# Seven products for a fourth quad of k tiles in the second pass of down, with splits in order of use and the LayerNorm's finishing steps put back

## The chip, the cores and the metric

The kernel runs on one core of one Trainium2 chip. The metric is the device time of one execution in microseconds (us). Below, PE is TensorE, DVE is VectorE, ACT is ScalarE, POOL is GpSimd and SP is SyncE; PEld is PE's loading of weights.

## The reference

One decoder layer on 256 tokens of width 2048, all in float32: a half-step FFN, a token mixer of two attention branches, a second half-step FFN, with a LayerNorm behind each. Cut to what matters here (D_MODEL 2048, D_FF 5632):

```python
def _swiglu(x, w_gate, w_up, w_down):
    return (jax.nn.silu(x @ w_gate) * (x @ w_up)) @ w_down

h = _layer_norm(ALPHA * h + 0.5 * _swiglu(h, ffn1_w_gate, ffn1_w_up, ffn1_w_down), ln1_g, ln1_b)
mix = _mixer(h, positions, ...)     # projections, MLA and differential attention, gates, w_out
h = _layer_norm(ALPHA * h + mix, ln2_g, ln2_b)
h = _layer_norm(ALPHA * h + 0.5 * _swiglu(h, ffn2_w_gate, ffn2_w_up, ffn2_w_down), ln3_g, ln3_b)
```

## The kernel before

**Three products for one.** Each float32 operand is split into a high part (a cast to `fp32r` by ACT, L150) and a low part (source minus high part, by DVE, L151). `triple` multiplies high by high (L203), high by the weight's low part (L204) and the activation's low part by the weight's high part (L205), each a PE instruction of 128 x 512, into one PSUM bank. Every weight tile is 128 x 1024 (two k tiles of 512 columns): one DMA from HBM into a `raw` or `sraw` tile, one cast and one subtraction into a pair of tiles called `wring`.

**The ring.** The `wring` pairs form a ring of six (four to five and more at other stages). `unit` queues a load, a preparation (the split) and the matmuls; `look(3, 4)` sets how many loads and how many splits stand ahead of the matmuls. A split can start only when the matmuls that read its pair before are done.

**Seven products.** Where two k tiles, two column halves and the two blocks of 128 tokens (b = 0, 1) can be taken as a 2 x 2 block product, seven products stand for eight, after Strassen's scheme. They need sums of weight tiles, made in place by DVE (`sraw<-sraw,sraw`, L392 in gate/up, L581 in down), and sums of activations (`f`, `xs`). In gate/up and in the mixer this is `Hybrid`, whose groups mix products of `sraw` tiles with plain units of `raw` tiles; `small` is the mixer's form of it. A group begins with product 1 on three pairs: `sraw`, `sraw`, `eraw`.

**Down.** The second matmul of the FFN has 44 k tiles, in 11 quads of four, and runs in two passes over the columns (p = 0, 1). `Sliced` takes some quads by seven products (seven units of one product, 6 matmuls each) and the others plainly (four units of 12 matmuls each). A string `mix` sets the order: `s` is a product, `p` a plain unit; eight plain units follow it. Before, quads 0 to 2 go by products in both passes. `QuadForms` holds a quad's split sums of `h`, `split_h` the plain splits of `h`. `hraw` tiles come from DRAM, where `turn_out` has written `h` transposed through `blocks` tiles.

**LayerNorm.** `evac` adds a bank to the row tile `z` (L729, L731) and takes its statistics (L734); after the last of four, `apply` aggregates them (L746), makes the inverse root (L645 to L662, the root itself on ACT, L647, with a table of functions to load first), and normalises the four pieces of `z` (L764, 128 x 512 each). PE transposes each piece (L633, to `tr`), ACT applies gain and bias by columns on the way out (L638) and casts to `h`: that is the input of the next stage. The rows for the residual get their gain and bias later, by DVE: the finishing steps L769 and L770, eight a block. `later(n, f)` calls `f` after n more units. The order in which the engines get their instructions is set by a scheduler that simulates the program's costs; `tc.issue_after(i)` keeps what is issued in its scope behind instruction i.

Of the kernel before, what the change touches and what calls it, by code (L numbers as in the profile page):

```python
# [59 lines left out]
def layer_kernel(ctx: ExitStack, tc: tile.TileContext, a: dict, out: bass.AP):  # L60
# [87 lines left out]

    def split(hi, lo, src):
        S.copy(hi, src)  # L150
        return V.tensor_tensor(out=lo, in0=src, in1=hi.bitcast(F32), op=ALU.subtract)  # L151
# [176 lines left out]

    class Hybrid:


        def __init__(self, x, seven, k_tiles, small=False, extra=None):

            self.x, self.seven, self.k_tiles, self.small, self.extra = x, seven, k_tiles, small, extra
            self.raws = {n: [act_tile([P, 1024], F32, "sraw") for _ in range(2)] for n in ("11", "12", "22")}
            self.raws["21"] = self.raws["12"] if small else [act_tile([P, 1024], F32, "sraw") for _ in range(2)]
            if extra is not None:
                for pair in (("11", "12"), ("22", "21")):
                    t = act_tile([P, 2, 512], F32, "eraw")
                    for i, n in enumerate(pair):  # L340
                        self.raws[n] = self.raws[n] + [t[:, i, :]]
            self.snaps = [act_tile([P, 2, 512], F32, "snap") for _ in range(2)]

        def group(self, w0, w1, done, wide=False, seeded=False):
# [36 lines left out]
            def seventh(p, s):  # L381
# [7 lines left out]
                def prep():  # L389
                    t = R[src][s]  # L390
                    if add is not None and (small or p != 7):
                        V.tensor_tensor(out=t, in0=t, in1=R[add[1]][s], op=ALU.add)  # L392
# [3 lines left out]
                    split(*pair, t)  # L396
# [16 lines left out]
            def plain(n, j, last=False):  # L413
# [8 lines left out]
                def prep():  # L422
                    pair = next_pair()
                    split(*pair, st["raw"])
                    st["pair"] = [v.rearrange("p (g n) -> p g n", g=G) for v in pair]

                def now():
# [7 lines left out]
                    if last:  # L435
                        done(1, 0, banks["Z"], n2, ALU.add)
                        done(1, 1, banks["X"], q5, ALU.add)
# [254 lines left out]
    class LayerNorm:  # L692
        def __init__(self, scale, residual, g, bt, each, x=None, cols=None, at=((0, 2, 4, 6), (8, 11, 14, 17))):
            self.scale = scale
            self.x = x
# [8 lines left out]
            self.gb = [[None, None] for _ in range(2)]  # L704

# [17 lines left out]
        def evac(self, c, b, bank):  # L723
            if c == 2 and b == 0:
                S.activation(sm(1, "sq"), zero[:, 0:1], AF.Sqrt)
# [18 lines left out]
        def apply(self, b):  # L744
# [18 lines left out]
            for c in range(4):  # L763
                V.tensor_scalar(out=zs[c], in0=zs[c], scalar1=mv[:, 0:1], scalar2=r,  # L764
                                op0=ALU.subtract, op1=ALU.mult)
                rows_to_quad(zs[c], b, self.x, c, *self.cols)

            def finish(c):
                V.tensor_tensor(out=zs[c], in0=zs[c], in1=gs[c], op=ALU.mult)  # L769
                V.tensor_tensor(out=zs[c], in0=zs[c], in1=bs[c], op=ALU.add)  # L770
                self.each(b, c, zs[c])
# [3 lines left out]
    def ffn(n, x, wgu, wdn, residual, g, bt, each, first=None, between=None, nxt=None, cols=None):  # L775
# [3 lines left out]
        def put_h(b, q):  # L779
            turn_out(hb[b, q], hT[q, b])  # L780

        def half(c, b, up, gate):
# [7 lines left out]
            if c % 2 == 1:  # L790
                later(2, lambda: put_h(b, q))
# [37 lines left out]
        def first_hook(j):  # L829
            if first is not None:  # L830
                first(j)
            if j == 5:
# [3 lines left out]
                between=between, behind_x=2 if n == 2 else None)  # L836
# [12 lines left out]
        ln = LayerNorm(0.5, residual, g, bt, each, nxt, cols, ((24, 26, 48, 50), (94, 97, 100, 103)))  # L849
# [3 lines left out]
        forms = {q: QuadForms(spare) for q in range(3)}  # L853
        down = Sliced(h_at)
# [5 lines left out]
        for p in range(2):  # L860
# [4 lines left out]
            else:  # L865
                kept = (9, 10)
                rest = deque(quad_units((9, 10, 3, 4)) + [(m, 2 * q + i) for m in range(2) for q in (5, 6, 7, 8) for i in range(2)])
                mix = "p" + "spspspspspspsppp" * 2 + "spspspspspss"
            products = deque((q, f, None) for q in range(3) for f in order)
# [7 lines left out]
            for q in range(3, KF // 4):  # L877
                first_use = min(i for i, u in enumerate(units) if len(u) == 2 and u[1] // 2 == q)
# [12 lines left out]
            else:  # L891
                call(len(units) - 8, widen)
# [507 lines left out]
```

## Time and profile before

| | |
|---|---|
| runs | 1984.77 us median of 3 (1983.05 to 1985.32) |
| profiled execution | 1982.88 us, its span 1981.1 |
| PE clock granted | 0.997 |
| sum of PE's idle time | 19.3 us |

The stages in the profiled execution: gate/up of the first FFN to about 440 us, down to 687 (its second pass from 572), the mixer to 1297, the second FFN to 1970, of which the second pass of down takes 1854 to 1970, and then the last LayerNorm. Times in profile lines are us from the span's start. In a timeline line the first number is the start, the second the duration; `x2` means two of the kind in a row; what stands in brackets is idle time before it and what ended it. In a line of the waits the numbers are the total, how many, and the longest. In a line of the windows stand the window, its length, the busy time of PE, PEld, DVE, ACT and POOL with their counts, the granted clock, the share of the DMA engines and GB/s. A PE instruction's duration goes on while the next has begun, so the pitch of matmuls is read from starts.

### The profile page before, as it was taken

The page shows a single profiled execution, that of the slowest core. Times are in us where ns is not written, and L with a number is a line of the kernel's source. Part 1 is how long each engine was busy: PE and PEld are TensorE (multiplying, and loading weights), DVE is VectorE, ACT ScalarE, POOL GpSimd, SP SyncE. Part 2 cuts the span into 40 slices and gives each one's busy share as a digit, 9 for nine tenths or more (in the row PEclk, how much of TensorE's full clock was granted, in tenths as well). Part 3 has the DMA queues.
Part 4 walks back from the last instruction along what each step waited for, and adds up shares of the span by engine and source line. Part 5 has one row for each costly group of instructions (what it writes and reads, how often), then busy time and mean ns, then how long its engine had stood idle before and what let it go on. Part 6 is the DMA issues. An engine that isn't in the chain of part 4 may idle for free.

```text
span 1981.1 us, 25579 instructions
## 1 busy us (share of the span) xinstructions
PE 1961.8 (99%) x8796; PEld 1623.6 (82%) x8796; DVE 1761.0 (89%) x2135; ACT 1269.4 (64%) x1639; POOL 294.6 (15%) x515
## 2 busy tenths in 40 slices
PE   9999999999999999999999999999999999999997
PEld 8888888888888897888888888878888888888886
DVE  7999999999898889998977686699999999998886
ACT  6666666677655666666667864566666666766552
POOL 0211112112100011002223130012112211121000
PEclk9999999999999999999999999999999999999999
DMA  8978888869677666677667677578898878687663
GB/s 314 284 241 279 284 238 247 239 212 329 244 235 243 202 243 225 226 254 260 217 198 256 216 236 264 185 256 271 244 290 260 247 239 244 208 325 251 238 215 124
DMA packets 144594, 484.63 MB, mean 245 GB/s; under 512 B 20640, under 2 KB 20688, under 8 KB 144464
## 3 DMA queue, kind: packets, MB, share of 16 engines
q1 hardware_dynamic: 112752, 389.60, 57.1%
q0 software_dynamic: 31712, 93.41, 17.9%
q8 instruction: 69, 1.13, 0.2%
q14 instruction: 61, 0.50, 0.1%
HBM read 454.08 MB, written 28.84 MB: 244 GB/s over the span
## 4 chain that ended last, share of the span: by engine, by line
PE 89%; DVE 6%; issue 3%; DMA 1%; POOL 0%; ACT 0%; SPq 0%; DVEq 0%; POOLq 0%; ACTq 0%
PE mm L204 28%; PE mm L205 28%; PE mm L203 28%; DVE wring L151 3%; DVE sraw L392 1%; PE tr L203 1%; PE tr L204 1%; PE tr L205 1%; DMA raw<-in_gu_dram 1%; PE tr L633 0%; DMA sraw<-in_wgm_dram 0%; PE tr L1134 0%; PE tr L1207 0%; PE tr L1209 0%; DMA hT<-blocks 0%
## 5 line engine op out<-in xcount | busy, mean ns | idle before, releaser
L150 ACT CAST wring<-raw 128x1024 fp32r<-128x1024 f32 (+2 forms) x475 | 491.4, 1038 | 344.9 <-PE mm L205 244.6
L151 DVE TENSOR_TENSOR wring<-raw,wring 128x1024 fp32r<-128x1024 f32 (+2 forms) x475 | 568.7, 1203 | 112.5 <-ACT wring L150 104.9
L150 ACT CAST wring<-sraw 128x1024 fp32r<-128x1024 f32 x436 | 455.4, 1052 | 207.7 <-PE mm L205 73.2
L151 DVE TENSOR_TENSOR wring<-sraw,wring 128x1024 fp32r<-128x1024 f32 x436 | 525.9, 1222 | 25.5 <-ACT wring L150 21.4
L205 PE MATMUL mm<-wring,h 128*128 128x512 f32 (+2 forms) x1260 | 485.0, 385 | 0.0
L203 PE MATMUL mm<-wring,h 128*128 128x512 f32 (+2 forms) x1260 | 484.7, 385 | 0.0
L204 PE MATMUL mm<-wring,h 128*128 128x512 f32 (+2 forms) x1260 | 484.6, 385 | 0.0
L204 PE MATMUL mm<-wring,xs 128*128 128x512 f32 x776 | 303.1, 391 | 2.5 <-DVE wring L151 2.4
L203 PE MATMUL mm<-wring,xs 128*128 128x512 f32 x776 | 302.3, 390 | 0.0
L205 PE MATMUL mm<-wring,xs 128*128 128x512 f32 x776 | 302.1, 389 | 0.0
L205 PEld LDWEIGHTS mm<-wring,h 128*128 128x128 f32 x1260 | 236.7, 188 | 47.4 <-DVE h L151 0.9
L203 PEld LDWEIGHTS mm<-wring,h 128*128 128x128 f32 x1260 | 236.9, 188 | 46.9 <-ACT h L150 0.4
L204 PEld LDWEIGHTS mm<-wring,h 128*128 128x128 f32 x1260 | 236.8, 188 | 46.9 <-DVE wring L151 0.3
L392 DVE TENSOR_TENSOR sraw<-sraw,sraw 128x1024 f32<-128x1024 f32 x168 | 203.3, 1220 | 3.5 <-DMA sraw<-in_wdv_dram 1.2
L204 PEld LDWEIGHTS mm<-wring,xs 128*128 128x128 f32 x776 | 145.6, 188 | 36.5 <-DVE wring L151 6.5
L203 PEld LDWEIGHTS mm<-wring,xs 128*128 128x128 f32 x776 | 145.7, 188 | 30.2
L205 PEld LDWEIGHTS mm<-wring,xs 128*128 128x128 f32 x776 | 145.7, 188 | 30.0
L204 PE MATMUL mm<-wring,x 128*128 128x512 f32 x348 | 135.7, 390 | 0.5 <-DVE wring L151 0.5
L203 PE MATMUL mm<-wring,x 128*128 128x512 f32 x348 | 135.7, 390 | 0.0
L205 PE MATMUL mm<-wring,x 128*128 128x512 f32 x348 | 135.2, 389 | 0.0
L394 POOL DMA_DIRECT2D sraw<-in_gu_dram x40 | 35.5, 887 | 579.0 <-DVE sraw L392 572.5
L670 POOL DMA_DIRECT2D hT<-blocks x176 | 97.2, 578 | 129.1 <-DVE blocks L668 117.6
(301 smaller groups left out, 2219.6 us busy)
## 6 DMA issues: line engine op xcount, KB each, us to landing
raw<-in_gu_dram SPq DMA_DIRECT2D x167, 512.0 KB, 4.9
sraw<-in_gu_dram SPq DMA_DIRECT2D x160, 512.0 KB, 5.1
raw<-in_dn_dram SPq DMA_DIRECT2D x140, 512.0 KB, 4.6
sraw<-in_gu_dram POOLq DMA_DIRECT2D x40, 512.0 KB, 5.5
sraw<-in_dn_dram SPq DMA_DIRECT2D x36, 512.0 KB, 5.4
hraw<-hT POOLq DMA_DIRECT2D x68, 256.0 KB, 5.3
raw<-in_w_out_dram SPq DMA_DIRECT2D x32, 512.0 KB, 4.4
eraw<-in_gu_dram SPq DMA_DIRECT2D x48, 256.0 KB, 5.1
```

Source lines behind the costliest of these rows:

```text
L150: S.copy(hi, src)
L151: return V.tensor_tensor(out=lo, in0=src, in1=hi.bitcast(F32), op=ALU.subtract)
L203: PE.matmul(o, xh, wh, start=first, stop=False, skip_group_check=again)
L204: PE.matmul(o, xh, wl, start=False, stop=False, skip_group_check=again)
L205: PE.matmul(o, xl, wh, start=False, stop=last, skip_group_check=again)
L392: V.tensor_tensor(out=t, in0=t, in1=R[add[1]][s], op=ALU.add)
L394: nc.gpsimd.dma_start(R["12"][s], source("22", s), accum_op=ALU.add)
L670: nc.gpsimd.dma_start(to.rearrange("(g r) (i f) -> i r g f", g=4, i=4)[i], t[32 * i:32 * (i + 1), :].rearrange("r (g f) -> r g f", g=4))
```

## The change

In the second pass of both downs the quad 3 (k tiles 12 to 15) goes by seven products as well. `mix` gets 28 products and 20 plain units for 21 and 24, in periods of 12 units for 16; with the eight at the end that is 56 units for 53. The forms of quad 3 are made in that pass, and those of quads 0 to 2 are given back behind their last product. Over the kernel PE has 12 matmuls of 512 columns fewer, DVE 28 instructions more (six splits and eight adds of 1024 columns among them), and ACT 26 table loads for 28.

The LayerNorm asks for the root's table ahead (`root_at` units after the second of the four evacuations of b = 1, behind the last cast). The finishing steps of both blocks stand behind the normalising step of b = 1 (`applied[1]`). In the hybrid groups outside the mixer each split stands behind the one before it (`split_in_line`), and the adds behind one or two of them; the writing out of `h` comes two units later and behind the last split.

```diff
+    line = []
+    def behind_split(n):
+        return tc.issue_after(line[-n].ins) if len(line) >= n else nullcontext()
+    def split_in_line(strict, *a):
+        with behind_split(1) if strict else nullcontext():
+            line.append(split(*a))
...
                     if add is not None and (small or p != 7):
-                        V.tensor_tensor(out=t, in0=t, in1=R[add[1]][s], op=ALU.add)
+                        with nullcontext() if small else behind_split(s + 1):
+                            V.tensor_tensor(out=t, in0=t, in1=R[add[1]][s], op=ALU.add)
...
-                    split(*pair, t)
+                    split_in_line(not small, *pair, t)
...
         def evac(self, c, b, bank):
-            if c == 2 and b == 0:
-                S.activation(sm(1, "sq"), zero[:, 0:1], AF.Sqrt)
+            def root_table():
+                with tc.issue_after(cast[0].ins):
+                    S.activation(sm(1, "sq"), zero[:, 0:1], AF.Sqrt)
+            if c == 1 and b == 1:
+                later(self.root_at, root_table)
...
             def finish(c):
-                V.tensor_tensor(out=zs[c], in0=zs[c], in1=gs[c], op=ALU.mult)
-                V.tensor_tensor(out=zs[c], in0=zs[c], in1=bs[c], op=ALU.add)
+                with tc.issue_after(self.applied[1].ins):
+                    V.tensor_tensor(out=zs[c], in0=zs[c], in1=gs[c], op=ALU.mult)
+                    V.tensor_tensor(out=zs[c], in0=zs[c], in1=bs[c], op=ALU.add)
...
             if c % 2 == 1:
-                later(2, lambda: put_h(b, q))
+                later(4, lambda: put_h(b, q))
...
-                between=between, behind_x=2 if n == 2 else None)
+                between=between, behind_x=3 if n == 2 else None)
...
+        late = (3,)
...
-                rest = deque(quad_units((9, 10, 3, 4)) + [(m, 2 * q + i) ...])
-                mix = "p" + "spspspspspspsppp" * 2 + "spspspspspss"
+                rest = deque(quad_units([q for q in (9, 10, 3, 4) if q not in late]) + [(m, 2 * q + i) ...])
+                mix = "p" + "sspspsspspsp" * 3 + "sspspspsps"
-            products = deque((q, f, None) for q in range(3) for f in order)
+            products = deque((q, f, None) for q in (range(3) if p == 0 else (0, 1, 2) + late) for f in order)
```

Three places show what moves. The first is DVE at the start of a gate/up group of the first FFN: adds and splits before, then the same after. `sraw` and `eraw` are the tiles of product 1, `raw_1155` is that of the plain unit behind it.

```order
L392 TENSOR_TENSOR sraw_460<-sraw_460,sraw_464 128x1024
L392 TENSOR_TENSOR sraw_461<-sraw_461,sraw_465 128x1024
L392 TENSOR_TENSOR eraw_468<-eraw_468,eraw_469 128x512
L151 TENSOR_TENSOR wring_121<-raw_1155,wring_120 128x1024
L151 TENSOR_TENSOR wring_115<-sraw_460,wring_114 128x1024
L151 TENSOR_TENSOR wring_105<-sraw_461,wring_104 128x1024
L151 TENSOR_TENSOR wring_103<-eraw_468,wring_102 128x512
```

```order
L405 TENSOR_TENSOR sraw_460<-sraw_460,sraw_464 128x1024
L405 TENSOR_TENSOR sraw_461<-sraw_461,sraw_465 128x1024
L405 TENSOR_TENSOR eraw_468<-eraw_468,eraw_469 128x512
L153 TENSOR_TENSOR wring_115<-sraw_460,wring_114 128x1024
L153 TENSOR_TENSOR wring_105<-sraw_461,wring_104 128x1024
L153 TENSOR_TENSOR wring_103<-eraw_468,wring_102 128x512
L153 TENSOR_TENSOR wring_121<-raw_1155,wring_120 128x1024
```

The split of `raw_1155` has moved from ahead of the three to behind them.

The second is DVE in the second LayerNorm, from the last evacuation of b = 1 (`z_9770`, after: `z_9784`) to the normalising step; `wring` rows are splits of the second FFN's first weights.

```order
L729 TENSOR_TENSOR z_9770<-mm_10163,z_9770 128x512
L151 TENSOR_TENSOR wring_105<-raw_10496,wring_104 128x1024
L734 BN_STATS bn_9643<-z_9770 128x6
L151 TENSOR_TENSOR wring_103<-raw_10517,wring_102 128x1024
L746 BN_AGGR mv_10359<-bn_9643 128x2
L770 TENSOR_TENSOR z_9664<-z_9664,gb_9913 128x512
L645 TENSOR_SCALAR ve_10361<-mv_10359 128x1
L769 TENSOR_TENSOR z_9735<-z_9735,gb_9863 128x512
L649 TENSOR_SCALAR w_10365<-mv_10359 128x1
L653 RECIPROCAL y_10367<-sd_10363 128x1
L770 TENSOR_TENSOR z_9735<-z_9735,gb_9966 128x512
L656 SCALAR_TENSOR_TENSOR t_10369<-y_10367,w_10365 128x1
```

```order
L749 TENSOR_TENSOR z_9784<-mm_10177,z_9784 128x512
L754 BN_STATS bn_9657<-z_9784 128x6
L153 TENSOR_TENSOR wring_117<-raw_10531,wring_116 128x1024
L766 BN_AGGR mv_10373<-bn_9657 128x2
L659 TENSOR_SCALAR ve_10375<-mv_10373 128x1
L663 TENSOR_SCALAR w_10379<-mv_10373 128x1
L667 RECIPROCAL y_10381<-sd_10377 128x1
L670 SCALAR_TENSOR_TENSOR t_10383<-y_10381,w_10379 128x1
L676 SCALAR_TENSOR_TENSOR f_10385<-t_10383,y_10381 128x1
L784 TENSOR_SCALAR z_9706<-z_9706,mv_10373,f_10385 128x512 x2
L784 TENSOR_SCALAR z_9784<-z_9784,mv_10373,f_10385 128x512 x2
L790 TENSOR_TENSOR z_9678<-z_9678,gb_9820 128x512 x2
```

The finishing steps (L769, L770) are gone from between the aggregate and the normalising step, and a split from ahead of the aggregate.

The third is DVE in the second pass of the first down, after: the third quad of products begins. `sraw_3452` is the tile that products 1, 5, 6 and 4 read and add to, `raw_4760` to `raw_4839` are plain units and the `21` tile; PE uses the pairs in the order `wring_105`, `103`, `121`, `119`, `117`, `115`.

```order
L153 TENSOR_TENSOR wring_105<-sraw_3452,wring_104 128x1024
L153 TENSOR_TENSOR wring_121<-raw_4760,wring_120 128x1024
L595 TENSOR_TENSOR sraw_3452<-sraw_3452,sraw_3453 128x1024
L153 TENSOR_TENSOR h_5028<-hraw_4925,h_5027 128x512
L595 TENSOR_TENSOR sraw_3453<-sraw_3453,sraw_3454 128x1024
L153 TENSOR_TENSOR wring_117<-raw_4794,wring_116 128x1024
L153 TENSOR_TENSOR wring_103<-sraw_3452,wring_102 128x1024
L153 TENSOR_TENSOR wring_115<-sraw_3453,wring_114 128x1024
L595 TENSOR_TENSOR sraw_3452<-sraw_3452,sraw_3454 128x1024
L153 TENSOR_TENSOR wring_105<-raw_4822,wring_104 128x1024
L153 TENSOR_TENSOR wring_103<-raw_4839,wring_102 128x1024
L153 TENSOR_TENSOR wring_119<-sraw_3452,wring_118 128x1024
```

The split of product 5 (`wring_103`) stands behind those of two later plain units, and the split of product 6 (`wring_119`) behind those of four pairs that PE uses later.

38 lines of the change are left out of this document (28 added, 10 removed).

## The prediction

> **What bounds the kernel now.** I read the page first, for the engine that carries the chain.
>
> ```profile
> span 1981.1 us, 25579 instructions
> PE 1961.8 (99%) x8796; PEld 1623.6 (82%) x8796; DVE 1761.0 (89%) x2135; ACT 1269.4 (64%) x1639; POOL 294.6 (15%) x515
> PE 89%; DVE 6%; issue 3%; DMA 1%; POOL 0%; ACT 0%; SPq 0%; DVEq 0%; POOLq 0%; ACTq 0%
> ```
>
> TensorE is the bound almost everywhere: only fewer matmuls, or fewer stalls of PE, can shorten the kernel. VectorE at 89% stands close behind, so whatever gives it work needs a look at the place where it lands. Next came the waits of PE, to see which stalls there are at all.
>
> ```profile
> PE tr L633 <- DVE z L764: 4.1, 1, 4.1
> PE mm L204 <- DVE wring L151: 3.0, 8, 1.3
> ```
>
> So there is one wait of 4.1 us for a LayerNorm's normalised rows, and eight for the low half of a weight split, the longest 1.3. The rest of the 19 us between PE's busy time and the span lies at the end, behind the last matmul, where the change leaves the last LayerNorm's work as it is. The third view is the timeline at those waits. This is the first of the eight, where a group of gate/up products begins; the columns are start, duration, engine and instruction.
>
> ```profile
> 142.56 1.22 DVE L151 TENSOR_TENSOR wring<-raw,wring 128x1024 fp32r<-128x1024 f32 x1
> 143.70 2.36 DVE L151 TENSOR_TENSOR wring<-sraw,wring 128x1024 fp32r<-128x1024 f32 x2
> 143.94 0.39 PE L204 MATMUL mm<-wring,x 128*128 128x512 f32 x1
> 144.17 0.39 PE L205 MATMUL mm<-wring,x 128*128 128x512 f32 x1
> 144.40 0.39 PE L203 MATMUL mm<-wring,xs 128*128 128x512 f32 x1
> 144.98 0.50 PE L204 MATMUL mm<-wring,xs 128*128 128x512 f32 x1 [0.19 <-DVE wring L151]
> 145.31 0.39 PE L205 MATMUL mm<-wring,xs 128*128 128x512 f32 x1
> ```
>
> Two prices come from it. A 512-column matmul lasts 0.39 us, but the next starts 0.23 later (143.94, 144.17, 144.40): I price matmuls by that pitch, 0.227 over longer stretches. A split of 1024 columns keeps VectorE for 1.14 (142.56 to 143.70). And the stall, shown as 0.19, costs more: 144.40 to 144.98 is 0.35 above the pitch, 144.98 to 145.31 another 0.10, so 0.45.
>
> **The matmuls.** Six PE instructions of 512 columns go with each b and k tile by the plain way, 48 for a quad; the seven products take 42. Two FFNs: 12 fewer, times 0.227 = **-2.7 us**, if PE stays the bound. By the full 0.39 it would be 4.7, a bound I don't use since starts are 0.23 apart.
>
> **Splits in order of use.** At 142.56 the split of a `raw` tile, which PE wants only after the seven's first products, runs ahead of the split of `sraw`, which PE waits for at 144.98. After the change the three `sraw` and `eraw` splits come first: theirs is done 1.14 us sooner, which is more than the 0.45 it came late. What it delays, the `raw` split, comes 2.9 us later (two splits of 1.14 and one of 0.6), at 146.7 instead of 143.8, and is wanted behind the 15 matmuls of the first product, at 144.40 + 0.45 + 15 x 0.227 = 148.3: it stays in time. Of the eight waits the longest, 1.3, belongs to the mixer's small group, whose order the change keeps. The seven others vanish: 7 x 0.45 = **-3.2 us**, 0 to -3.4. The adds that make the later products now stand in twos and threes behind the splits (2.3 to 3.4 us of VectorE in one piece); I cost that at nothing, since the ring keeps splits several us ahead there. If that cover were gone, each group would lose up to one add, 1.14.
>
> **The second LayerNorm.** These are VectorE and PE around the 4.1 us wait, then the window with its granted clock.
>
> ```profile
> 1288.94 0.69 DVE L729 TENSOR_TENSOR z<-mm,z 128x512 f32<-128x512 f32 x1
> 1292.59 0.26 DVE L746 BATCH_NORM_AGGREGATE mv<-bn 128x2 f32<-128x24 f32 x1
> 1292.76 0.63 DVE L770 TENSOR_TENSOR z<-z,gb 128x512 f32<-128x512 f32 x1
> 1296.15 1.92 DVE L764 TENSOR_SCALAR z<-z,mv,f 128x512 f32<-128x512 f32 x4
> 1299.31 1.29 DVE L769 TENSOR_TENSOR z<-z,gb 128x512 f32<-128x512 f32 x2
> ...
> 1292.29 0.39 PE L205 MATMUL mm<-wring,h 128*128 128x512 f32 x1
> 1296.75 3.37 PE L633 MATMUL tr<-ident,z 128*128 128x128 f32 x16 [4.07 <-DVE z L764]
> 1299.86 0.79 PE L203 MATMUL mm<-wring,h 128*128 128x512 f32 x1
> 1300.45 0.56 PE L204 MATMUL mm<-wring,h 128*128 128x512 f32 x1
> ...
> 1290.00:1300.00 10.00, 5.93 (x29) 4.60 (x27) 9.88 (x22) 3.90 (x10) 2.14 (x4) 0.87 0.77 279
> ...
> 685.32 0.20 ACT L647 ACTIVATE sd<-ve 128x1 f32<-128x1 f32 x1
> 686.21 1.92 DVE L764 TENSOR_SCALAR z<-z,mv,f 128x512 f32<-128x512 f32 x4
> ```
>
> From the last evacuation (1288.94) to the normalising step (1296.15) VectorE takes 7.2 us. Five finishing steps of the first block (gain and bias, L769 and L770) stand between the aggregate (1292.59) and the normalising step, 3.6 us later. The change puts them behind it; what is left is the root's own chain, 0.9 from the root to the normalising step where nothing is in between (the last two rows, of the first LayerNorm) and some 0.5 up to the root, an estimate from the short instructions around it: 1.4, so 2.2 less. One of the two splits between the evacuation and the aggregate is put ahead of both, another 1.1. So 7.2 becomes 3.9, and PE's wait of 4.1 becomes about 0.8. Behind the stall the clock is down: 0.87 over those ten us, and the first matmul at 1299.86 is followed only after 0.59. Without that another 0.7 goes, 0.4 of it in that gap. Together 4.0. The rule of the Trainium skill's page "TensorE: Matmul & The Clock Gate" (The HAM clock gate) says that an idle window of about 3.4 us halves the clock for about as long. The trace agrees with it, 4.07 us idle and then the lower clock; by that rule a wait of 0.8 would leave the clock up, as the sum has it.
>
> Not all of it can stay, for VectorE is busy without a pause until 1319 and the next weight splits are hardly ahead of PE:
>
> ```profile
> 1310.15 1.22 DVE L151 TENSOR_TENSOR wring<-raw,wring 128x1024 fp32r<-128x1024 f32 x1
> 1311.79 0.62 PE L204 MATMUL mm<-wring,h 128*128 128x512 f32 x2
> ```
>
> That split ends at 1311.37; the second of the two matmuls, which reads it, starts at 1312.01: 0.64 ahead. PE may come sooner by 0.64 plus what VectorE comes sooner. Before, 13 finishing steps stand between the evacuation and that split, after it 10, 0.60 each (two in 1.29 at 1299.31): 1.8, and the split put ahead 1.1. That makes 3.5, and less where an added instruction waits: I take **-3.2** (0 to -4.0). The six left over fall between later splits that have 4 us in hand.
>
> **The root's table.** In its first block the switch of tables stands in front of the root:
>
> ```profile
> 1273.67 1.28 ACT L647 ACT_TABLE_LOAD   x1
> ```
>
> PE has other matmuls there and no wait in the list above, so its 1.28 earlier costs and brings nothing. The page "ScalarE: Activation LUTs" of the Trainium skill (What ACT_TABLE_LOAD costs) has 1.28 us for the load too, but 2.66 with a drain; here the next instruction started at 1274.96, so no drain is seen, and by its figure too the saving would be hidden.
>
> **The first LayerNorm.** Here the change takes something away. Now four matmuls of the old pass and more stand between its transposes and the first use of `h`:
>
> ```profile
> 686.90 1.51 PE L633 MATMUL tr<-ident,z 128*128 128x128 f32 x12
> 688.16 0.48 PE L205 MATMUL mm<-wring,h 128*128 128x512 f32 x1
> 689.55 0.95 PE L203 MATMUL mm<-wring,h 128*128 128x512 f32 x2
> ...
> 687.57 1.51 ACT L638 ACTIVATE h1raw<-tr,cols 128x128 f32<-128x128 f32 x4 [0.16 <-PE tr L633]
> 689.30 0.64 ACT L150 CAST h<-h1raw 128x512 fp32r<-128x512 f32 x1
> ```
>
> ScalarE needs 3.0 us from the first transpose (686.90) to the end of the cast (689.94). After the change 16 transposes stand in one piece, 1.7 us by the 12 in 1.26 here, and the matmul that reads `h` is next: a wait of 1.3, and some 0.3 for the low half. The detours of now cost PE about 0.6 (689.55 and on): **+1.0** (0.3 to 2.0).
>
> **The fourth quad on VectorE.** In each second pass VectorE gets three splits and four adds of 1024 columns (7 x 1.14), four subtractions and its own splits of `h` less the plain ones, 2.3 together: 10.3 us. The quads of products also follow faster: 12 units where there were 16, 23.1 us of PE (7 products of 1.36, 5 plain of 2.72) for 34. The windows are the units before the last eight, of the first FFN and the second; below them are three splits there, and the matmuls that read them.
>
> ```profile
> 572.00:666.00 94.00, 94.00 (x417) 77.82 (x416) 84.97 (x105) 56.66 (x61) 4.37 (x8) 1.00 0.70 232
> 1854.00:1948.00 94.00, 94.00 (x417) 77.82 (x416) 80.97 (x81) 52.24 (x55) 4.25 (x8) 1.00 0.67 229
> ...
> 631.00 1.22 DVE L151 TENSOR_TENSOR wring<-raw,wring 128x1024 fp32r<-128x1024 f32 x1 [1.49 <-ACT wring L150]
> 636.02 1.22 DVE L151 TENSOR_TENSOR wring<-raw,wring 128x1024 fp32r<-128x1024 f32 x1
> 650.99 1.22 DVE L151 TENSOR_TENSOR wring<-raw,wring 128x1024 fp32r<-128x1024 f32 x1
> ...
> 640.82 0.39 PE L204 MATMUL mm<-wring,h 128*128 128x512 f32 x1
> 644.90 0.39 PE L204 MATMUL mm<-wring,h 128*128 128x512 f32 x1
> 657.14 0.39 PE L204 MATMUL mm<-wring,h 128*128 128x512 f32 x1
> ```
>
> VectorE would do 95.3 of 92.6 us in the first FFN, 91.3 in the second: it lives on its lead. The last quad of now is already packed as all will be, and there the lead falls from 7.7 (636.02, done 637.24, read 644.90) to 4.9 (done 652.21, read 657.14): 2.7 a quad. Four such quads use 10.8 of a lead of 7.7, so the first FFN comes 3.1 us short; the order of the change fits, for it puts the splits of later plain units ahead of those of two earlier products in the third quad. In the second VectorE has 4.0 less to do and just holds. **+3.1** (0 to 7).
>
> **Sum.** -2.7 - 3.2 - 3.2 + 1.0 + 3.1 = -5.0. The profiled execution took 1982.88 (span 1981.1 and 1.8 around it), so about 1977.9; the median of the runs lies 1.9 higher, so I say 1979.8.
>
> **Rivals.** *No new stall in the second pass*: the lead holds, as the 8.6 at 631.00 (done 632.22, read 640.82) and the 1.49 of idle before it suggest; -8.1, 1976.7. Against it stands VectorE's sum above PE's. *The LayerNorm gives nothing*: VectorE stays as late at 1310 as now, since the same finishing steps come in one piece before those splits; the 3.2 is lost, 1983.0. For it speaks the lead of 0.64, against it the three steps and the split that leave. *Slower: the second pass runs on VectorE in both FFNs.* If a quad costs 3.7 of lead, as from 631.00 to 650.99 (8.6 to 4.9), and from order and loads rather than load on VectorE, so that the second FFN pays too, the shortfall is 2 x (4 x 3.7 - 7.7) = 14.2, and -8.1 becomes +6.1: 1990.9. It is slower than before from a loss of 2.95 a quad on, and by over 0.2% from 3.45. Against it: the loss read over the nearer pair is 2.7, and VectorE has 13 us free in the second FFN.
>
> **Chances.** Forecast 0.46, no new stall 0.17, LayerNorm for nothing 0.17, slower 0.13, something else 0.07. A measurement of this kernel tells 0.2%, 4.0 us, from no change. Two thirds of the forecast's own spread, the second case and some of the rest lie below 1980.8: 0.53 faster. The rest of the forecast and the third case are within: 0.33. Slower 0.14. The range goes from 1975.0, the second case with the LayerNorm's 4.0 and the lower end of the first LayerNorm, to 1987.0, the third case with 4 us more in the second pass; half of the slower case and the odd ones are left out.
>
> **What would show it.** Right: no wait of PE for L151 at the groups' starts; PE's wait before the transposes near 1290 at 0.3 to 1.5, the granted clock there 1.00; a wait of 1 to 1.5 before the first `h` behind the first LayerNorm; PE waits for `wring` splits near 620 to 660 of some 3 us, none near 1900. Wrong: waits over 5 us in those passes, waits in the middle of the gate/up groups, or the first matmuls of the second FFN's gate held up by their splits for as long as the LayerNorm gained.

## The result and the profile after

The changed kernel takes **1995.4 us** (median of six runs, 1993.25 to 1996.95), the kernel before 1984.28 beside it: the ratio is 1.0057, with a 95% interval of 1.0047 to 1.0067. It is slower by 11 us, where 4.6 faster was forecast. The profiled execution took 1994.21, its span is 1992.4. (In the diff above the last part of `mix` lacks one letter; the program has "sspspsspsps".)

The page of after, with the engines and the chain:

```profile
span 1992.4 us, 25630 instructions
PE 1964.7 (99%) x8784; PEld 1623.6 (81%) x8784; DVE 1774.8 (89%) x2163; ACT 1268.0 (64%) x1649; POOL 294.3 (15%) x515
PE 80%; DVE 11%; issue 4%; DMA 3%; ACT 1%; POOL 0%; SPq 0%; DVEq 0%; ACTq 0%; POOLq 0%
```

PE has its 12 matmuls fewer and yet is busy 3 us longer: some of them ran at a lower clock. The chain has moved by 9% of the span from PE to DVE, issue and DMA. PE's waits in after:

```profile
PE tr L647 <- DVE z L784: 5.0, 2, 4.6
PE tr L206 <- DVE wring L153: 4.2, 2, 2.4
PE mm L206 <- DVE wring L153: 2.8, 5, 1.2
PE tr L205 <- ACT wring L152: 1.8, 1, 1.8
```

The wait of 4 us for a LayerNorm's rows is still there, but at another LayerNorm. New are the waits of `tr` matmuls, which are products of the second pass of down.

**The second pass of the first FFN.** The timeline of after there, first PE, then ScalarE and VectorE, then SyncE's issue of loads, then the window:

```profile
624.83 0.49 PE L205 MATMUL tr<-wring,xs 128*128 128x512 f32 x1 [1.83 <-ACT wring L152]
627.76 0.80 PE L206 MATMUL tr<-wring,xs 128*128 128x512 f32 x1 [2.44 <-DVE wring L153]
628.36 0.63 PE L207 MATMUL tr<-wring,xs 128*128 128x512 f32 x1
628.78 0.63 PE L205 MATMUL tr<-wring,xs 128*128 128x512 f32 x1
...
619.12 1.05 ACT L152 CAST wring<-sraw 128x1024 fp32r<-128x1024 f32 x1 [6.27 <-DMA sraw<-in_dn_dram]
623.73 1.04 ACT L152 CAST wring<-sraw 128x1024 fp32r<-128x1024 f32 x1 [0.62 <-DVE sraw L595]
...
611.06 2.35 DVE L153 TENSOR_TENSOR wring<-sraw,wring 128x1024 fp32r<-128x1024 f32 x2
620.20 1.23 DVE L153 TENSOR_TENSOR wring<-sraw,wring 128x1024 fp32r<-128x1024 f32 x1 [2.58 <-ACT wring L152]
622.48 1.22 DVE L595 TENSOR_TENSOR sraw<-sraw,sraw 128x1024 f32<-128x1024 f32 x1
624.22 1.22 DVE L595 TENSOR_TENSOR sraw<-sraw,sraw 128x1024 f32<-128x1024 f32 x1
625.35 1.22 DVE L153 TENSOR_TENSOR wring<-raw,wring 128x1024 fp32r<-128x1024 f32 x1
626.49 2.35 DVE L153 TENSOR_TENSOR wring<-sraw,wring 128x1024 fp32r<-128x1024 f32 x2
...
612.30 1.46 SPq L590 DMA_DIRECT2D sraw<-in_dn_dram  x2
...
606.00:640.00 34.00, 29.73 (x119) 23.78 (x118) 28.19 (x34) 17.76 (x22) 2.12 (x4) 0.90 0.69 243
```

Read it from the load. One tile holds block 11 of the weights, and products 1, 5, 6 and 4 use it in turn, adding to it in place. The next quad's load can be issued only when the split for product 4 is done, at 612.30; the cast for the next product 1 waits 6.27 us on ScalarE and starts at 619.12, 6.8 after the issue. PE reaches that product just as its split ends (621.4), so the load has cost it nothing yet. What it waits for is the next product, 5: its add follows only at 622.48, and PE waits 1.8 for the cast behind that add (623.73); then an add for product 7 (624.22) and the split of a plain unit (625.35) stand in VectorE's line ahead of its split (626.49), and PE waits 2.4. So the late load takes away the lead, and the order that the third view of the change showed, six us from product 1's split to product 5's, then lies open. VectorE is not short of time here: in the window it is busy 28.19 of 34 us. Behind 4.3 us of waiting the matmuls come 0.43 apart for a while (628.36, 628.78) instead of 0.23: the granted clock in that window is 0.90, before it was 1.00. The waits cost 4.7 us of PE's starts and the lower clock 2.5: 7.2 there. In the second FFN the same place costs 4.0, with one wait, and matmuls 0.43 apart behind it:

```profile
1916.17 0.66 PE L206 MATMUL tr<-wring,xs 128*128 128x512 f32 x1 [1.80 <-DVE wring L153]
1916.62 0.63 PE L207 MATMUL tr<-wring,xs 128*128 128x512 f32 x1
1917.05 0.63 PE L205 MATMUL tr<-wring,xs 128*128 128x512 f32 x1
```

**The first LayerNorm.** The same three engines:

```profile
698.84 3.80 PE L647 MATMUL tr<-ident,z 128*128 128x128 f32 x16 [4.64 <-DVE z L784]
702.69 0.79 PE L205 MATMUL mm<-wring,h 128*128 128x512 f32 x1
...
693.26 1.05 ACT L152 CAST wring<-raw 128x1024 fp32r<-128x1024 f32 x1 [3.69 <-DMA raw<-in_wc_dram]
694.22 0.19 ACT L661 ACTIVATE sd<-ve 128x1 f32<-128x1 f32 x1
...
691.40 0.15 DVE L663 TENSOR_SCALAR w<-mv 128x1 f32<-128x1 f32 x1
694.34 1.23 DVE L153 TENSOR_TENSOR wring<-raw,wring 128x1024 fp32r<-128x1024 f32 x1 [2.80 <-ACT wring L152]
695.49 0.15 DVE L667 RECIPROCAL y<-sd 128x1 f32<-128x1 f32 x1
698.15 1.91 DVE L784 TENSOR_SCALAR z<-z,mv,f 128x512 f32<-128x512 f32 x4
```

The root (694.22) stands on ScalarE behind the cast of a tile of `in_wc`, the mixer's first weights, which waits 3.69 for its load. VectorE then runs three splits of that matrix between the root's steps. So a weight that PE wants much later holds up the LayerNorm for which PE is waiting, and after 4.64 us of idle PE runs at half clock again (16 transposes in 3.80, the first matmuls 0.59 and 0.43 apart).

**The second LayerNorm** did what was forecast:

```profile
1305.47 0.39 PE L207 MATMUL mm<-wring,h 128*128 128x512 f32 x1
1306.25 1.57 PE L647 MATMUL tr<-ident,z 128*128 128x128 f32 x12 [0.39 <-DVE z L784]
1308.51 0.66 PE L647 MATMUL tr<-ident,z 128*128 128x128 f32 x4 [0.69 <-ACT h2raw L652]
1309.36 0.50 PE L205 MATMUL mm<-wring,h 128*128 128x512 f32 x1 [0.20 <-ACT h L152]
```

The wait is 0.39 for 4.07, and PE's last matmul of the mixer to the first of the FFN takes 3.9 us (1305.47 to 1309.36) for 7.6 (1292.29 to 1299.86): 3.7 gained.

Where the 11 us are, from PE's times at the same instructions in both traces: gate/up of the first FFN -0.1, its second pass of down +6 (7.2 less 1.4 of matmuls), the first LayerNorm +7, the mixer +0.5, the second LayerNorm -3.7, gate/up of the second FFN -0.2, its pass +2.6 (4.0 less 1.4), the rest -0.5: 11.3 together.

### The profile page after: what moved, and what is told of

Same layout as the page of the kernel before. It is cut to its first block, busy times and chain, and to the rows that moved or that the text cites. A ratio compares the mean times of both kernels' runs of the same rounds, so it can differ in the third digit from the quotient of the medians.

```text
span 1992.4 us, 25630 instructions
## 1 busy us (share of the span) xinstructions
PE 1964.7 (99%) x8784; PEld 1623.6 (81%) x8784; DVE 1774.8 (89%) x2163; ACT 1268.0 (64%) x1649; POOL 294.3 (15%) x515
## 4 chain that ended last, share of the span: by engine, by line
PE 80%; DVE 11%; issue 4%; DMA 3%; ACT 1%; POOL 0%; SPq 0%; DVEq 0%; ACTq 0%; POOLq 0%
PE mm L206 25%; PE mm L207 25%; PE mm L205 25%; DVE wring L153 6%; DMA sraw<-in_dn_dram 2%; DVE sraw L405 1%; ACT wring L152 1%; DVE sraw L595 1%; PE tr L206 1%; PE tr L207 1%; DMA raw<-in_wc_dram 1%; PE tr L205 1%; DVE blocks L682 1%; PE tr L647 0%; DMA sraw<-in_wgm_dram 0%
## 5 line engine op out<-in xcount | busy, mean ns | idle before, releaser
L152 ACT CAST wring<-raw 128x1024 fp32r<-128x1024 f32 (+2 forms) x469 | 483.6, 1037 | 316.8 <-PE mm L207 204.6
L153 DVE TENSOR_TENSOR wring<-raw,wring 128x1024 fp32r<-128x1024 f32 (+2 forms) x469 | 559.4, 1199 | 104.7 <-ACT wring L152 103.1
L152 ACT CAST wring<-sraw 128x1024 fp32r<-128x1024 f32 x448 | 464.3, 1051 | 232.5 <-DVE sraw L405 77.7
L153 DVE TENSOR_TENSOR wring<-sraw,wring 128x1024 fp32r<-128x1024 f32 x448 | 535.5, 1218 | 40.5 <-ACT wring L152 39.3
L205 PE MATMUL mm<-wring,h 128*128 128x512 f32 (+2 forms) x1228 | 472.9, 386 | 0.2 <-ACT h L152 0.2
L207 PE MATMUL mm<-wring,h 128*128 128x512 f32 (+2 forms) x1228 | 473.1, 386 | 0.0
L206 PE MATMUL mm<-wring,h 128*128 128x512 f32 (+2 forms) x1228 | 472.9, 385 | 0.0
L206 PE MATMUL mm<-wring,xs 128*128 128x512 f32 x792 | 309.1, 390 | 2.7 <-DVE wring L153 2.0
L205 PE MATMUL mm<-wring,xs 128*128 128x512 f32 x792 | 308.5, 389 | 0.0
L207 PE MATMUL mm<-wring,xs 128*128 128x512 f32 x792 | 308.3, 389 | 0.0
L206 PEld LDWEIGHTS mm<-wring,h 128*128 128x128 f32 x1228 | 231.6, 189 | 46.6 <-DVE wring L153 1.1
L205 PEld LDWEIGHTS mm<-wring,h 128*128 128x128 f32 x1228 | 231.6, 189 | 46.4 <-ACT h L152 0.9
L207 PEld LDWEIGHTS mm<-wring,h 128*128 128x128 f32 x1228 | 231.2, 188 | 46.1 <-DVE h L153 0.5
L206 PEld LDWEIGHTS mm<-wring,xs 128*128 128x128 f32 x792 | 148.7, 188 | 36.8 <-DVE wring L153 6.1
L205 PEld LDWEIGHTS mm<-wring,xs 128*128 128x128 f32 x792 | 148.6, 188 | 30.9
L207 PEld LDWEIGHTS mm<-wring,xs 128*128 128x128 f32 x792 | 148.7, 188 | 30.6
```

The lines of the kernel that those rows point to most:

```text
L152: cast[0] = S.copy(hi, src)
L205: PE.matmul(o, xh, wh, start=first, stop=False, skip_group_check=again)
L206: PE.matmul(o, xh, wl, start=False, stop=False, skip_group_check=again)
L207: PE.matmul(o, xl, wh, start=False, stop=last, skip_group_check=again)
```

## The experiments

The times are medians, each ratio to the kernel before on the same chip. Theory R, the reload of shared tiles, and its rivals are told in the expectations.

| run | us | ratio, 95% interval |
|---|---|---|
| changed kernel | 1995.4 | 1.0057 (1.0047 to 1.0067) |
| e1 without the fourth quad | 1981.9 | 0.9991 (0.9982 to 1.0001) |
| e2 the fourth quad alone | 1995.9 | 1.0057 (1.0042 to 1.0072) |
| e3 two tiles for block 11 | 1993.1 | 1.0041 (1.0026 to 1.0056) |
| e4 splits free | 1995.9 | 1.0060 (1.0045 to 1.0075) |
| e5 two tiles for each block | 1987.0 | 1.0014 (1.0005 to 1.0023) |
| e6 one tile, gap in the order | 1986.1 | 1.0011 (1.0002 to 1.0021) |
| e7 LayerNorm part alone | 1982.7 | 0.9993 (0.9984 to 1.0002) |
| e8 no fourth quad, adds free | 1984.3 | 0.9998 (0.9989 to 1.0007) |
| e9 mixer's splits behind the LayerNorm | 1994.6 | 1.0052 (1.0035 to 1.0069) |
| e10 e6 with e9 | 1987.0 | 1.0019 (1.0010 to 1.0029) |
| e11 e5 with e6's order and e9 | 1986.3 | 1.0015 (1.0005 to 1.0025) |
| e12 fourth quad in the second FFN alone | 1982.5 | 0.9990 (0.9980 to 0.9999) |

**Which part it is.** e1 takes the quad out of the changed kernel, e2 puts it alone into the kernel before, with the making of its forms, and e4 frees the splits.

```diff
# e1, and for e2 the other way round in the kernel before
-        late = (3,)
+        late = ()
...
-                mix = "p" + "sspspsspspsp" * 3 + "sspspsspsps"
+                mix = "p" + "spspspspspspsppp" * 2 + "spspspspspss"
# e4
     def behind_split(n):
-        return tc.issue_after(line[-n].ins) if len(line) >= n else nullcontext()
+        return nullcontext()
...
-                later(4, lambda: put_h(b, q))
+                later(2, lambda: put_h(b, q))
...
-                between=between, behind_x=3 if n == 2 else None)
+                between=between, behind_x=2 if n == 2 else None)
```

> The changed kernel with the second pass of down as before (quad 3 plain, the old mix). Theory R (reload): the loss comes from the fourth quad, since the one tile that products 1, 5, 6 and 4 share is reloaded while PE waits, and the first LayerNorm's wait of 4.6 us follows from the lead lost there. Then this kernel has no wait in either second pass, under 1.5 us at the first LayerNorm, keeps the 3.7 us won at the second, and takes 1980 to 1982. Theory N (norm): the first LayerNorm's wait comes from the finishing steps and the table put elsewhere; then the wait of 4.6 and the half clock behind it stay, and it takes 1988 to 1990.

> The kernel before with the second pass of down alone changed (quad 3 by products, the new mix). Theory R: waits of 4 to 5 us near 620 and of 2 near 1910, with half clock behind them, and a wait at the first LayerNorm of some us; 1984.3 - 2.7 + 8 + 4 + up to 8, so 1993 to 2001. Theory N: the waits of the passes alone, no new one at the first LayerNorm: 1992 to 1994.

> The changed kernel without the order of splits (splits, adds and the writing out of h free for the scheduler, as before). By the prediction that order is worth 3.2 us: 1998.6. By the trace of after each group's stall only went from 0.45 to 0.28, because the adds start later by about as much as the split came forward: 0.5 to 1 us, 1995.4 to 1996.5, and less certain, for the scheduler may move other places.

e1 gave 1981.9, e2 1995.9: the quad alone is worth a loss of some 12 us, and the rest of the change is hardly 2 faster, a gain that e1's interval does not yet tell from none. Theory N as it was put is out: with the finishing steps put back but no quad, PE waits for normalised rows 0.9 us at two LayerNorms together, 0.5 at most. In e2 the first LayerNorm's wait is 1.4, and the second's 4.3 is kept. That e2 and the changed kernel take the same time is therefore chance: by PE's times at the same instructions e2 loses 7.4 in the first pass, 1.2 at the first LayerNorm and 3.9 in the second FFN's pass, the changed kernel 6.0, 6.8 and 2.6, less what it gains at the second LayerNorm. At the first LayerNorm the quad alone costs 1.2, the LayerNorm part without the quad (e1, e7) 1.3 to 1.7, both together 6.8.

```profile
PE mm L206 <- DVE wring L153: 2.8, 5, 1.2
PE tr L647 <- DVE z L784: 0.9, 2, 0.5
PE tr L647 <- ACT h1raw L652: 0.7, 1, 0.7
```

These are e1's waits; no `tr` matmul waits in the pass. e4 is as slow as the changed kernel: its time shows no worth of the order of splits, though intervals of 3 us to either side hardly rule out the 3.2 that I gave it. The traces do: gate/up of both FFNs takes 0.9 longer in e4, and 0.7 of that is one wait at 1719.

**The tiles.** e3 and e5 give a block a second tile, e6 keeps one and moves plain units.

```diff
# e5 (e3: for "11" alone)
-            self.R = {n: act_tile([P, 1024], F32, "sraw") for n in ("11", "12", "22")}
+            self.R = {n: [act_tile([P, 1024], F32, "sraw") for _ in range(2)] for n in ("11", "12", "22")}
...
-                        nc.sync.dma_start(R[load_block], w[j])
+                        nc.sync.dma_start(R[load_block][q % 2], w[j])
# e6
-                mix = "p" + "sspspsspspsp" * 3 + "sspspsspsps"
+                mix = "p" + "sspsspsssppp" * 3 + "sspsspsspps"
```

> The changed kernel with two tiles for the shared operand (block 11), used by turns, so that the next quad's load doesn't wait for the last add of the quad before. Theory R: both passes' waits and their half clock go (8 and 4 us), the lead at the pass's end is back to several us and the first LayerNorm's wait falls below 2: 1976 to 1980. Theory V (VectorE's work): the tile is not what binds, VectorE's 10.3 us more per pass is; then PE still waits for wring splits in the first FFN, and the time stays above 1990.

> The changed kernel with two tiles for each of the three blocks (11, 12, 22) that the products share, used by turns. Theory R2 (one tile each is too few for quads that follow every 23 us: with two for block 11 alone the wait moved on to block 22, where an add waited 2.7 us for its load): no wait over 0.6 in either pass, no half clock there, the first LayerNorm's wait at most 1: 1977 to 1981. Theory V (VectorE, or the load on DMA): waits of several us at wring splits stay in the first FFN, 1988 to 1993.

> The changed kernel with one tile each and the same units, in another order: products 1, 5, plain, 6, 7, plain, 2, 4, 3 and then three plain units, so that PE has 10.9 us instead of 8.2 between product 4 and the next product 1, and 15.0 instead of 9.5 between 3 and the next 6. Theory R2: the reload of either tile is hidden again, the waits in the passes go or fall below 1 us each, and it takes 1977 to 1983. Theory V: the work of VectorE, of ScalarE and of DMA is the same to the last instruction, so the waits stay and it takes 1990 to 1996.

e3 took the waits at 622 away and got another, 20 us earlier. VectorE in e3, an add for product 7 that waits for block 22's load, and PE's longest wait:

```profile
600.74 1.23 DVE L602 TENSOR_TENSOR sraw<-sraw,sraw 128x1024 f32<-128x1024 f32 x1 [2.67 <-DMA sraw<-in_dn_dram]
PE tr L206 <- DVE wring L153: 5.8, 5, 3.7
```

It is block 22's turn: products 6, 7 and 3 share that tile, and product 5's split, for which PE waits 3.7, stands behind that add in VectorE's line. The pass costs as much as in the changed kernel, 6.2 more than before. With two tiles for every block (e5) PE works through the first FFN's pass without a pause, VectorE as busy as it can be. Its windows over that pass:

```profile
572.00:606.00 34.00, 34.00 (x152) 28.15 (x151) 33.97 (x53) 21.76 (x23) 2.12 (x4) 1.00 0.61 204
606.00:640.00 34.00, 34.00 (x152) 28.15 (x151) 33.97 (x41) 24.99 (x32) 3.19 (x6) 1.00 0.73 255
640.00:676.00 36.00, 36.00 (x160) 29.84 (x159) 34.38 (x37) 19.71 (x21) 0.00 (x0) 1.00 0.58 195
```

Here the quad pays what was counted: by PE's times both second passes take 1.4 less than before, six matmuls each. Theory V, that VectorE's added work makes the stalls, does not fit with that, since e5 has all of it. The order of VectorE's work changed a little too: product 5's split stands behind one plain unit's instead of two, and what that adds is not told apart.

e6 points the same way without a byte more of memory: every unit of the changed kernel is there, in another order, and the ratio falls from 1.0057 to 1.0011. Its trace, of an execution of 1990.0 and so among its slowest, shows less: a wait of 1.8 and one of 1.5 are left in the first pass, 1.6 and 1.1 in the second FFN's, the granted clock from 606 to 640 is 0.95 for 0.90, and the passes cost 4.4 and 2.3 for 6.0 and 2.6. The waits did not fall below 1 there, as theory R2 had it; how they stand in e6's faster executions is not shown. So it is e5 that shows theory R2 for the passes. The totals, 1977 to 1983, were missed by 3 to 10 us: neither run gets below the kernel before.

**What is left.** e5, with a clean pass, still waited at the first LayerNorm, so I gave that a test of its own.

```diff
# e9
-        project(a["wc0"], x, KD, 512, cq_done)
+        project(a["wc0"], x, KD, 512, cq_done, behind_x=3)
```

> The changed kernel, but the mixer's first projection splits its fourth and later weight tiles behind the first LayerNorm's first normalised piece (casts and subtractions both), as the second FFN does it. Theory L: the 4.6 us wait there is the root, and the normalising step, standing in line on ScalarE and VectorE behind splits that wait for loads of in_wc, which come late since the lead is lost in the pass before. Then the wait falls to 1 or less and the half clock behind it goes; the passes' own waits stay: 1995.4 - 4 - 3 = 1988 to 1990. Theory P (PE reaches the LayerNorm with nothing left to do, whatever the order): the wait moves to the first matmuls of the mixer, 1994 to 1996.

> One tile each, three plain units behind product 3 (as in the run with the gap), and the mixer's later splits behind the first LayerNorm. Theory L: 1 to 1.5 us below the run with the gap alone: 1984.5 to 1985. Theory P: the same as that run, 1986.

> Two tiles for each block, the gap, and the mixer's later splits behind the first LayerNorm: each of the three found causes taken away. If these are all, no wait above 1 us is left between 572 and 700 and between 1854 and 1970, and the fourth quad shows its 2.7 us: 1979 to 1981, below the kernel without it (1981.9). If VectorE's 10 us a pass cost beyond that, 1983 to 1986.

In e9 the normalising step comes 1 us after PE is free, as meant, and the wait turns up one step later. PE, then ScalarE:

```profile
692.59 1.50 PE L647 MATMUL tr<-ident,z 128*128 128x128 f32 x12 [1.18 <-DVE z L784]
697.53 0.66 PE L647 MATMUL tr<-ident,z 128*128 128x128 f32 x4 [2.74 <-ACT h1raw L652]
...
695.02 1.04 ACT L152 CAST wring<-raw 128x1024 fp32r<-128x1024 f32 x1 [3.80 <-DMA raw<-in_wc_dram]
695.97 1.50 ACT L652 ACTIVATE h1raw<-tr,cols 128x128 f32<-128x128 f32 x4
```

Now the cast that waits for its load stands ahead of the activations that empty the transposes' bank. The head of line is the same, the load; only who stands behind it has changed, and the mixer waits for its splits in addition (1994.6). So theory P was the better one. e10, which adds e9 to e6, took 1987.0, no less than e6, and speaks for P too. The loads are late. The first load of `in_wc` is issued 23.6 us before PE ends the pass in the kernel before (663.19 to 686.77), 18.2 in e5 (669.81 to 687.98) and 17.3 in after (676.88 to 694.21). In e5 VectorE is behind by what the quad gave it to do, and a `raw` tile is free for the next load only when its split is done.

The lost lead is not the whole of it, though. In e2 the first load of `in_wc` is issued at 679.45, only 15.4 us before PE ends the pass, and PE waits 1.4. The load of the tile ahead of the root landed there in 4.4 us (687.40 to 691.82); the same tile's in after took 7.4 (685.74 to 693.16). In after, a load of 512 KB for the mixer, `gain`, is issued 0.8 us ahead of it and lands beside it, at 692.97; in e2, as in the kernel before, it comes behind a store of the residual's rows. GpSimd in after, then in e2:

```profile
684.98 0.53 POOL L1053 DMA_DIRECT2D gain<-in_c_gain_dram  x1 [46.84 <-PE mm L207]
...
702.94 0.54 POOL L1031 DMA_DIRECT2D gain<-in_c_gain_dram  x1
```

With the finishing steps put back those stores come later, and `gain` slips in front of them. In e1 and e7 this does little, for the load behind `gain` lands in 4.3 and 5.0 us, and the first six tiles of `in_wc` have landed before it is issued. That fits with 1.2 and 1.3 to 1.7 becoming 6.8, but no run moves this load alone, so it is not shown as the cause.

e11 takes all three causes away. There is no wait above 0.3 in the first FFN's second pass and none above 0.6 at its LayerNorm, as forecast, and the second FFN's second pass takes 1.4 less than before, as in e5. But the profiled execution, at 1990.6 one of its slower ones, gives it back elsewhere: waits for weight splits in the mixer's first 110 us (1.0, 0.8 and 1.7), and four of 0.5 to 1.3 in the second FFN's first pass, 1797 to 1818. The mixer takes some 5 more than in the kernel before, that first pass 7.5. The first kind I take to be the lead lost again. The second kind is there in e5 also (2.9 there) and in no run with one tile for each block; I take it to be the price of the added tiles, which come out of the same pool. Both were only argued. 1986.3: the quad's 2.7 us come through in the passes and not in the total.

> The changed kernel with the fourth quad in the second FFN only. By the trace of after the second FFN's pass loses 4.0 to its waits and half clock and gains 1.4: 2.6 above the kernel without the quad (1981.9), so 1984.5; the first FFN and the LayerNorm behind it then hold the rest, some 11 us. If instead each FFN has half of the loss, 1988 to 1989.

e12 has the quad in the second FFN alone: 1982.5, 0.6 above e1 and within what the two intervals leave open, where 2.6 was expected. By its trace the pass costs 0.6, for 2.6 in after and 3.9 in e2. VectorE has the same instructions in the same order there in e12 and in after. These are the cast behind the reload, PE's wait and the window behind it in e12, then the cast and the window in after, whose wait of 1.80 is shown above:

```profile
1898.90 1.05 ACT L152 CAST wring<-sraw 128x1024 fp32r<-128x1024 f32 x1 [5.77 <-DMA sraw<-in_dn_dram]
1905.94 0.50 PE L206 MATMUL tr<-wring,xs 128*128 128x512 f32 x1 [1.01 <-DVE wring L153]
1905.00:1908.00 3.00, 2.06 (x9) 1.73 (x10) 2.97 (x3) 0.82 (x1) 0.00 (x0) 1.00 0.38 143
...
1909.14 1.05 ACT L152 CAST wring<-sraw 128x1024 fp32r<-128x1024 f32 x1 [6.59 <-DMA sraw<-in_dn_dram]
1916.00:1919.00 3.00, 2.83 (x7) 2.28 (x8) 2.97 (x4) 1.59 (x2) 0.00 (x0) 0.56 0.18 67
```

The load was issued at 1891.31 in e12 and at 1900.72 in after, so it took 7.5 us and 8.4 to land. With 0.8 us more of load PE waits 0.8 longer (1.80 for 1.01), and the granted clock behind the wait is 0.56 where it stayed at 1.00: 2.1 us of difference for 0.8.

So nearly all of the loss is the first FFN's. There the pass carries other work of VectorE and other loads (the tables that the mixer needs), which no run took away, and the LayerNorm behind it is followed by weights whose loads come late; in the second FFN the last LayerNorm ends the kernel, with no weights behind it.

**The parts that help.**

```diff
# e8, on e1
-                        with nullcontext() if small else behind_split(s + 1):
+                        with nullcontext():
                             V.tensor_tensor(out=t, in0=t, in1=R[add[1]][s], op=ALU.add)
```

> The kernel before with the LayerNorm part alone (root's table ahead, finishing steps put back). By the trace of after: -3.7 at the second LayerNorm, +1 to +2 at the first: 1981.5, 0.2 to 0.1% faster than before. By the prediction -3.2 and +1.0: the same within 0.5. If the second LayerNorm's gain needs the other parts, no change.

> Second pass as before, LayerNorm part and splits in order as changed, but the adds of the gate/up groups free for the scheduler. If the group's stall stayed at 0.28 because the strict adds stand behind a split that waits for its pair, the stall now goes (7 x 0.28 = 2 us below the same kernel with strict adds): 1980. If the splits' order itself is what cannot gain, the stalls stay or turn up at the group's second product, and the time is that of strict adds, 1982.

e7, the LayerNorm part alone, is 1982.7: about 1 us faster, its interval just reaching no change. e8 is inconclusive: its profiled execution, at 1981.5 the fastest of its runs, has no stall left at the start of the groups that had one (0.28 with strict adds, 0.12 without, the wait 0), so the strict adds did hold them; but a new wait of 1.6 stands in the second FFN (near 1343), and its median is 1984.3, not below e1's.

## Why the prediction was wrong

**The matmuls**: 12 fewer, as counted; PE's instructions went from 8796 to 8784.

**The fourth quad on VectorE** is the step that failed. It was sized by adding up the lead that each quad uses: +3.1 in the first FFN, nothing in the second. Measured are +6.0 and +2.6, and most of the +7 at the first LayerNorm needs the quad too. The lead was the right thing to look at, and the place was right (622 to 631, the third quad, whose splits the order showed turned round). What I put as "it lives on its lead" was taken as a sum, though: VectorE's work against PE's. What bound it was a chain through one tile: four products in turn on the same operand, then a load of 6.8 us (4.2 to 5.4 in the kernel before) that cannot be issued until the last of them is split. The sum has no load in it, and the lead was read from the splits of plain units (631.00, 636.02, 650.99), which use no shared tile. With two tiles for each block both passes came out at -1.4, VectorE's work being the same. Before, PE had 13.6 us between product 4 and the next product 1 (two products and four plain units, by the prices above), and the reload was hidden; the new order left 8.2. ScalarE's waits show that the load has come onto the path. After, one line is new; the kernel before has no line for that load among its waits:

```profile
ACT wring L152 <- DMA sraw<-in_dn_dram: 26.2, 6, 6.6
```

They don't show its price: e12 has three such waits, 13.5 together, and its pass loses 0.6.

The rival for the slower side had "order and loads rather than load on VectorE", got 0.13 and 1990.9, and it too was sized as a lost lead that turns into a wait of the same length, 7.1 in each FFN. Measured are 7.2 in the first pass, 2.5 of it the lower clock behind the waits, and 4.0 in the second, so that the 7.1 meets the first is luck. That was the second omission: I priced half clock only where I had seen it, at the second LayerNorm, and not behind the stalls that I forecast myself. The Trainium skill's page "TensorE: Matmul & The Clock Gate" (The HAM clock gate), which the prediction cites for a gain, bears on stalls too: it has the clock fall after an idle window of about 3.4 us. The trace agrees at 694, where 4.64 us of waiting are followed by the lower clock. It does not at the other two places: at 623 waits of 1.83 and 2.44, with a matmul between, and in the second FFN a single wait of 1.80 were followed by matmuls 0.43 apart too, which that figure does not give; behind the 1.01 of e12 the clock stayed up.

**The first LayerNorm**: +1.0 forecast, about +7 measured with the quad, +1.7 without it (the LayerNorm part alone). The wait behind the transposes is there in e1 (0.7 and 0.2, as a wait in the middle of them and one for the cast). What I did not see is that the lead lost in the pass is paid a second time there: loads follow splits, splits stand ahead of the root on engines that work in order. It takes the LayerNorm part as well: the quad alone (e2) pays 1.2. No term of the sum joined two stages, or two parts of the change.

**Splits in order of use**: -3.2 forecast, -0.3 by the trace. In after the group begins so:

```profile
141.34 2.35 DVE L405 TENSOR_TENSOR sraw<-sraw,sraw 128x1024 f32<-128x1024 f32 x2
144.21 2.35 DVE L153 TENSOR_TENSOR wring<-sraw,wring 128x1024 fp32r<-128x1024 f32 x2
145.49 0.50 PE L206 MATMUL mm<-wring,xs 128*128 128x512 f32 x1
```

The split of `sraw` comes first now, but the adds in front of it start later: they stand behind the split of the tile before, which waited for its pair. VectorE gained 1.14 and lost nearly as much; the wait went from 0.19 to 0.12, the excess from 0.45 to 0.39 (0.28 and then 0.11). And of the seven waits that I counted, only six stand at groups' starts; the seventh is in the kernel's first matmuls, at 10.7 us, and stayed (0.53 before, 0.52 after). I had read in the order what the split is now ahead of, and not what its adds are now behind.

**The second LayerNorm**: -3.2 forecast, -3.7 measured in after; e1 keeps the short wait of 0.4, and in e7, the LayerNorm part alone, it is 1.8, so some of the gain came with the other parts. VectorE's later splits held.

**The root's table**: nothing, as forecast; no wait that names it.

The range's lower end sums to 1975.2, not 1975.0. Its upper end, 1987.0, left out half of the one rival that pointed the right way, and no case had the passes and the first LayerNorm fail together.

## What to carry to other kernels

When units follow faster, look for tiles with one buffer: count the time from the last use of a tile to its next, on the engine that sets the pace, and hold it against load, cast and split; an average of work per engine does not show it. A lead that is lost in one stage can be paid again in the next, where in-order engines put the next stage's late loads ahead of the step that everyone waits for. Take two parts of a change apart before adding their prices: here 1.2 and 1.3 to 1.7 became 6.8. And a stall can cost more than its length while PE's clock recovers: 2.5 us behind 4.3 here.

## What the runs showed that I had not expected

The same instructions in another order of units (e6) differ by 9 us. Some kernels with the quad in the first FFN scatter more: e6's ten runs lie from 1981.5 to 1990.6, those of the LayerNorm part alone within 1.3 us. A load that lands 0.8 us sooner or later, with the clock up or down behind it, can do part of that, as e12 beside after shows; that it does is not shown. And the half clock needs no long stall: eight matmuls at 0.43 us followed a wait of 1.80 in the second FFN (from 1916.17 on).
